# Four whole-array matmuls that nothing reads, at each level of the first ten triangular inverses

## The chip, the cores and the metric

The kernel runs on one NeuronCore of a Trainium2 chip. Its engines are TensorE (PE in the rows, with PEld for its weight loads), VectorE (DVE), ScalarE (ACT), GpSimd (POOL) and SyncE (SP), which issues the DMAs. The metric is the device time of one execution in microseconds. The kernel before takes 2458.19 us, the median of three runs that lie between 2457.12 and 2461.14 us.

## The reference

The reference is a two-layer backbone over 1024 latent and 256 context tokens of width 1024, in float32. Each layer normalizes and modulates its tokens, multiplies them by one input matrix, sends half of the columns through a retention group and half through an RWKV-7 group, gates both, multiplies by an output matrix and adds the result to the residual. What matters here is the recurrence of the RWKV group, which runs in both directions over 8 heads of 64 channels:

```python
def step(s, inp):
    r_t, w_t, k_t, v_t, kap_t, a_t = inp
    s_kap = jnp.einsum('bhvk,bhk->bhv', s, kap_t)
    s = (s * w_t[:, :, None, :]
         - s_kap[..., None] * (kap_t * a_t)[:, :, None, :]
         + v_t[..., None] * k_t[:, :, None, :])
    return s, jnp.einsum('bhvk,bhk->bhv', s, r_t)
```

The kernel computes it in chunks of 64 tokens. Within a chunk the recurrence is a triangular system, so each chunk needs the inverse of a 64x64 unit triangular matrix for every head and direction. That inverse depends on the inputs alone and not on the running state, so it can be made ahead of the scan.

## The kernel before

A layer has 4 pairs of heads (NP) and 10 steps (NT) for each pair. One step g covers 128 tokens, that is two chunks of 64 (index i) in two directions (index d) for two heads (index h), and the text below calls it a chunk, as the short description of the change does. So there are 40 chunks in a layer and 80 in the program. A chunk passes three functions:

- `prep` loads its features and makes the decayed vectors `own` and `bk`, mostly on DVE, ACT and POOL.
- `prep2` multiplies them (L962, tile `pm`), masks the products, and inverts the triangular part in six levels, n = 0 to 5, and three correction sums. The inverse lives in one bank of PSUM, the tile `pinv` of 512 columns (`pc` in the code). Its first half `q` takes the first products of a level (L1001: weights `hi`, moving operand `tz`, four matmuls with 64 columns each). DVE multiplies `q` by a mask into `xx` (L1015). The second half `tp` takes the second products (L1017: weights `ttb`, moving operand `xx`). ACT copies `tp` into the next `tz` (L1018), DVE turns it (L1021), ACT and POOL copy the result into `ttb` (L986), and the next level begins. After level 5 the sums of L990 and L993 follow. Two banks (LANES) let two chunks be inverted at a time.
- `seq` runs the recurrence itself over the chunk (L1053 and L1061, tile `pseq`).

Beside this scan a layer has a large amount of other PE work, which the text calls the fill: the input projections (L493 to L495), small products for the decay (L725), the retention group, and the output projection (L821 to L823). A generator hands out the fill in pieces. `ahead(g)` issues `prep` of chunk g and `prep2` of chunk g-1. At the start of a layer, `ahead` runs for g = 0 to LOOK (3), with 5 us of fill (RAMP) after each. From then on each step issues `seq`, `ahead(g + LOOK + 1)` and a share of the fill. All this fixes the order in which instructions are written down. A scheduler that simulates the engines then sets the order on each engine; `seq` and `prep2` stand under `tc.high_priority(offset=1000)`, so that it takes them before the fill where both are ready. On the chip each engine works through its list in that order.

Of the kernel before, what the change touches and what calls it, by code (L numbers as in the profile page):

```python
# [42 lines left out]
LOOK = 3  # L43
# [15 lines left out]
XB = 4  # L59
DENSE = ((447.0, 113.0), (403.0, 88.0))  # L60
DUE = (30, 37)


def shape_constants():
# [61 lines left out]
def hybrid_kernel(ctx: ExitStack, tc: tile.TileContext, a: dict, out: bass.AP, dbg: dict | None = None):  # L126
    nc = tc.nc
# [11 lines left out]
    def bank(tag, name):  # L139
        return ps.tile([128, 512], F32, tag=tag, name=name, bufs=BANKS[tag])  # L140
# [6 lines left out]
    def behind(ins, first):  # L147
        tc.add_manual_dep(ins.ins, first.ins.name, mybir.DependencyInfo(mybir.DependencyClass.NoSync, mybir.DependencyReason.DATA),
                          reason="the first product of a bank clears its written bits")
# [15 lines left out]
    def x_tile(tb):  # L165
        t = ln_pool.tile([128, D], F32, tag="xt", name="xt", bufs=XTB)
        load(t, a["ctx"][0, 128 * tb:128 * tb + 128, :] if tb < 2 else a["x"][0, 128 * (tb - 2):128 * (tb - 2) + 128, :])
        return t
# [20 lines left out]
    one16 = const.tile([128, 128], F16, name="one16")  # L189
# [37 lines left out]
    def turn(key):  # L227
        at[key] += 1
        return ring[key][(at[key] - 1) % len(ring[key])]
# [144 lines left out]
    for l in range(DEPTH):  # L374
# [55 lines left out]
        if l == 0:  # L430
            lp = ln_pool
            stage = [lp.tile([128, 8, 128 * len(tiles)], F32, name=f"xs{ci}") for ci, tiles in enumerate(LN_TILES)]
            for ci, tiles in enumerate(LN_TILES):
# [5 lines left out]
                for i, tb in enumerate(tiles):  # L439
                    t = x_tiles[tb] if tb < XTB else x_tile(tb)  # L440
# [7 lines left out]
                for k in range(8):  # L448
                    p = bank(("inv", "m")[k % 2], "pxt")
# [497 lines left out]
                nc.gpsimd.tensor_tensor(own[:, :, :, 64:128], rx, dt(exc(ep)), ALU.mult)  # L947
            return dict(s=s, uv=uv, f=f, own=own, bk=bk, skip_y=skip_y)

        def prep2(sp, c):  # L950
            own, bk, skip_y = c["own"], c["bk"], c["skip_y"]

            q1 = 64 if skip_y else 128
            gq = sp.tile([128, 2, 2, 2, 128], F32, tag="gq", name="gq", bufs=LIVE)
            bt = sp.tile([128, 2, 2, 128], F32, tag="bt", name="bt", bufs=LIVE)
            quad = lambda t: t.rearrange("p (i d t) -> p i d t", i=2, d=2)
            pm = {}
            for h in range(2):
                pm[h] = quad(bank("m", f"pm{h}"))
                for i in range(2):  # L960
                    for d in range(2):
                        nc.tensor.matmul(pm[h][:, i, d, 0:q1], bk[HR[h], i, d, :], own[HR[h], i, d, 0:q1],  # L962
                                         start=True, stop=True)
                for i in range(2):
                    nc.vector.tensor_tensor(gq[:, h, i, :, 0:q1], pm[h][:, i, :, 0:q1], m1mask[:, :, 0:q1], ALU.mult)  # L965
            pt = quad(bank("m", "pbt"))
            for i in range(2):
                for d in range(2):
                    nc.tensor.transpose(pt[:, i, d, :], bk[:, i, d, :], ident)
            nc.scalar.activation(bt, pt, AF.Copy, scale=rowf)  # L970

            hi, lo = turn("hi"), turn("lo")
            idb = ident[0:64, 0:64].unsqueeze(1).unsqueeze(1).to_broadcast([64, 2, 2, 64])
            il = sp.tile([128, 2, 2, 64], F32, tag="il", name="il", bufs=1)
            for h in range(2):
                nc.gpsimd.tensor_tensor(il[HR[h]], gq[0:64, h, :, :, 0:64], idb, ALU.add)  # L976
                nc.scalar.copy(hi[HR[h], :, :, 64 * h:64 * h + 64], il[HR[h]])  # L977
            lane = at["lane"] = (at["lane"] + 1) % LANES
            pc = bank("inv", "pinv")
            q, tp = [pc[:, 256 * k:256 * k + 256].rearrange("p (i d t) -> p i d t", i=2, d=2) for k in range(2)]  # L980
            ID = [(i, d) for i in range(2) for d in range(2)]
            idr = lambda t: t.rearrange("p i d t -> p (i d) t")

            def spread(dst, src):
                for h, eng in enumerate((nc.scalar.copy, nc.gpsimd.tensor_copy)):
                    eng(idr(dst[HR[h], :, :, 64 * h:64 * h + 64]), idr(src[HR[h]]))  # L986

            def one_sum(lhs, rhs, parts):

                one = nc.tensor.matmul(pc[:, 0:256], lhs, rhs, start=True, stop=False, skip_group_check=True)  # L990
                for n, (w, x) in enumerate(parts):
                    for i, d in ID:
                        behind(nc.tensor.matmul(q[:, i, d, :], w[:, i, d, :], x[:, i, d, :], start=False,  # L993
                                                stop=n == len(parts) - 1, skip_group_check=True), one)


            tz = ttb = tt = None
            for n in range(6):
                tzn = sp.tile([128, 2, 2, 64], F16, tag=f"tz{lane}", name="tz", bufs=2)
                for i, d in ID:  # L1000
                    nc.tensor.matmul(q[:, i, d, :], hi[:, i, d, :], id16 if n == 0 else tz[:, i, d, :], start=True, stop=True)  # L1001
                mk = lvm[:, :, n, :].unsqueeze(1).to_broadcast([128, 2, 2, 64])
                if n == 0:
                    nc.vector.tensor_tensor(tzn, q, mk, ALU.mult)
                    ttn = turn(f"ttb{lane}")
                    for d in range(2):
                        mt = lvm[:, 1 - d, 0, :].unsqueeze(1).unsqueeze(1).to_broadcast([128, 2, 2, 64])
                        nc.gpsimd.tensor_tensor(ttn[:, :, d, :].rearrange("p i (h t) -> p i h t", h=2),  # L1008
                                                hi[:, :, d, :].rearrange("p i (h t) -> p i h t", h=2), mt, ALU.mult)
                    for h in range(2):  # L1010
                        cols = slice(64 * h, 64 * h + 64)
                        nc.gpsimd.tensor_tensor(lo[HR[h], :, :, cols], il[HR[h]], hi[HR[h], :, :, cols], ALU.subtract)  # L1012
                else:
                    xx = sp.tile([128, 2, 2, 64], F16, tag=f"xx{lane}", name="xx", bufs=1)
                    nc.vector.tensor_tensor(xx, q, mk, ALU.mult)  # L1015
                    for i, d in ID:
                        nc.tensor.matmul(tp[:, i, d, :], ttb[:, i, d, :], xx[:, i, d, :], start=True, stop=True)  # L1017
                    nc.scalar.copy(tzn, tp)  # L1018
                    if n < 5:
                        tt = sp.tile([128, 2, 2, 64], F16, tag=f"tt{lane}", name="tt", bufs=1)  # L1020
                        nc.vector.transpose(idr(tt), idr(tzn))  # L1021
                        ttn = turn(f"ttb{lane}")
                        spread(ttn, tt)
                    else:
                        for d in range(2):
                            for h in range(2):
                                dn, up = [slice(64 * h + 32 * k, 64 * h + 32 * k + 32) for k in (1 - d, d)]
                                nc.vector.transpose(tt[up, :, d, 32 * (1 - d):32 * (1 - d) + 32], tzn[dn, :, d, 32 * d:32 * d + 32])
                tz, ttb = tzn, ttn
            one_sum(neg16, id16.unsqueeze(1).to_broadcast([128, 4, 64]), [(hi, tz), (lo, tz)])  # L1030
            e = turn("eb")
            for h in range(2):
                nc.scalar.activation(idr(e[HR[h], :, :, 64 * h:64 * h + 64]), idr(q[HR[h]]), AF.Copy, scale=-1.0)
            flat = lambda t: t.rearrange("p i d t -> p (i d t)")
            one_sum(one16, flat(tt), [(e, tt)])
            z1 = sp.tile([128, 2, 2, 64], F16, tag="z1", name="z1", bufs=1)
            nc.scalar.copy(z1, q)
            one_sum(one16, flat(tt), [(e, z1)])
            z2 = sp.tile([128, 2, 2, 64], F32, tag="z2", name="z2", bufs=ZB)
            nc.scalar.copy(z2, q)  # L1040
            c.update(gq=gq, bt=bt, z2=z2)
# [179 lines left out]
        def pump(w):  # L1221

            while w > 0 and fills:
                w -= take()

        def deal(g):

            n = len(fills)
            if n == 2 or (n == 1 and g >= DUE[0]):
                pump(left[-n] / max(DUE[-n] - g, 1))  # L1230

        def need(p, done):
            while p not in done:
                take()

        sp = open_pool("scan", other)
# [5 lines left out]
        stages, late = {}, {}  # L1242

        def ahead(g):
            p, s = divmod(g, NT)
            if p < NP:
                need(p, ready)
                stages[g] = prep(sp, p, s)
            if 0 <= g - 1 < NP * NT:
                with tc.high_priority(offset=1000):  # L1250
                    prep2(sp, stages[g - 1])

        for g in range(LOOK + 1):
            ahead(g)
# [2 lines left out]
        for p in range(NP):  # L1257
            st, ys = None, {}
            for s in range(NT):
                g = p * NT + s  # L1260
# [55 lines left out]
```

## Time and profile before

| | |
|---|---|
| time, median of 3 runs | 2458.19 us |
| the profiled execution, its own time | 2462.74 us |
| its span, first to last instruction | 2460.7 us |
| mean granted TensorE clock over the span | 0.964 of full speed |
| busy share of PE, DVE, ACT, POOL | 93%, 71%, 57%, 54% |
| DMA, mean over the span | 123 GB/s |

Line numbers are those of the kernel before. The busy time of PE counts a matmul from its start to its modelled end, so matmuls that follow one another closely overlap in it, and a stretch in which PE is shown as busy throughout can still run at either clock. A granted clock of 1.00 is 2.4 GHz and one of 0.50 is 1.2 GHz; a mean between the two is a stretch with some of both. A bracket at the end of a timeline row gives the idle time of the engine before that row and what ended it.

### The profile page before, as it was taken

Reading aid. Unit: us, or ns where it says so; the run is one execution under the profiler, and the core shown is the slowest. Engines: PE = TensorE matmul, PEld = TensorE weight load, DVE = VectorE, ACT = ScalarE, POOL = GpSimd, SP = SyncE. Lnnn points to the kernel's source line nnn. Section 1 sums busy time; section 2 is a strip of 40 time slices with the busy share of each in tenths; the row PEclk is TensorE's granted clock in tenths of the full one; section 3 lists DMA queues with packets and bytes.
Section 4 is the critical chain, followed back from the end, with each engine's and each line's share of the span. In section 5 each row is a group of like instructions: output and inputs, shape, how many; then the busy total and the mean of one; then the engine's idle time right before and its main releaser. Section 6 shows DMA issues by size and latency. Waiting matters only on the chain.

```text
span 2460.7 us, 69593 instructions
## 1 busy us (share of the span) xinstructions
PE 2299.2 (93%) x25463; PEld 1739.9 (71%) x25463; DVE 1735.6 (71%) x4784; ACT 1414.8 (57%) x4261; POOL 1319.7 (54%) x2032
## 2 busy tenths in 40 slices
PE   5779999999999999999997899999999999998997
PEld 2357776877788777778655687778768877776855
DVE  2646686787678867777648677767867886669756
ACT  3455664565566655456546666646655665456663
POOL 1455564465556654456536556545654665456662
PEclk7888999999999999999998899999999999999998
DMA  8754443334334423335533543434433443334544
GB/s 313 270 187 110 117 118 87 113 108 124 78 89 139 126 70 92 75 100 154 176 108 123 152 130 112 108 94 119 128 87 100 124 124 80 79 88 120 143 130 128
DMA packets 539606, 302.77 MB, mean 123 GB/s; under 512 B 238995, under 2 KB 526465, under 8 KB 537217
## 3 DMA queue, kind: packets, MB, share of 16 engines
q1 hardware_dynamic: 539264, 298.33, 42.1%
q8 instruction: 201, 3.29, 0.6%
q14 instruction: 141, 1.15, 0.2%
HBM read 212.21 MB, written 85.98 MB: 121 GB/s over the span
## 4 chain that ended last, share of the span: by engine, by line
PE 58%; DVE 13%; DMA 6%; ACT 4%; issue 3%; POOL 2%; SPq 2%; DVEq 0%; POOLq 0%; ACTq 0%
PE pproj L493 8%; PE pproj L495 8%; PE pproj L494 8%; PE pseq L1061 8%; PE pm L962 5%; DMA ft<-feat 2%; PE pseq L1053 2%; PE pinv L1001 2%; PE pinv L1017 2%; PE pout L821 1%; PE pout L823 1%; PE pss L638 1%; PE pout L822 1%; PE pss L648 1%; PE pyt L1127 1%
## 5 line engine op out<-in xcount | busy, mean ns | idle before, releaser
L493 PE MATMUL pproj<-h_hi,whi 128*128 128x256 f16 (+2 forms) x2128 | 631.3, 298 | 9.1 <-ACT craw L505 5.1
L494 PE MATMUL pproj<-h_lo,whi 128*128 128x256 f16 (+2 forms) x2128 | 629.1, 297 | 7.6 <-DVE h_lo L365 7.1
L495 PE MATMUL pproj<-h_hi,wlo 128*128 128x256 f16 (+2 forms) x2128 | 627.2, 297 | 0.7 <-POOL wlo L320 0.7
L320 POOL TENSOR_TENSOR wlo<-wraw,whi 128x256 f16<-128x256 f32 x360 | 250.5, 707 | 208.7 <-ACT wraw L319 181.0
L495 PEld LDWEIGHTS <-wlo 128*128 128x128 f16 x2128 | 213.5, 100 | 76.5 <-issue 12.1
L494 PEld LDWEIGHTS <-whi 128*128 128x128 f16 x2128 | 212.6, 100 | 77.6 <-issue 18.6
L493 PEld LDWEIGHTS <-whi 128*128 128x128 f16 x2128 | 213.1, 100 | 75.3 <-issue 10.4
L986 POOL COPY ttb<-tt 64x256 f16<-64x256 f16 x320 | 139.1, 436 | 205.2 <-DVE tt L1021 160.5
L1015 DVE TENSOR_TENSOR xx<-pinv,lvm 128x256 f16<-128x256 f32 x400 | 164.3, 416 | 90.6 <-PE pinv L1001 87.4
L318 ACT ACTIVATE whi<-wraw 128x256 f16<-128x256 f32 x360 | 139.2, 412 | 132.9 <-PE pproj L494 61.1
L1018 ACT CAST tz<-pinv 128x256 f16<-128x256 f32 x400 | 146.1, 370 | 119.9 <-PE pinv L1017 107.7
L962 PE MATMUL pm<-own,bk 64*128 64x128 f32 (+1 forms) x1280 | 201.6, 294 | 8.3 <-DVE bk L942 4.0
L1021 DVE STREAM_TRANSPOSE tt<-tz 128x256 f16<-128x256 f16 x320 | 139.4, 437 | 97.0 <-ACT tz L1018 94.3
L976 POOL TENSOR_TENSOR il<-gq,c_id 64x256 f32<-64x256 f32 x160 | 120.1, 751 | 133.1 <-DVE gq L965 119.3
L986 ACT COPY ttb<-tt 64x256 f16<-64x256 f16 x320 | 128.6, 402 | 106.5 <-DVE tt L1021 102.1
L962 PEld LDWEIGHTS pm<-own,bk 64*128 64x128 f32 x1280 | 163.2, 193 | 33.1 <-issue 8.6
L965 DVE TENSOR_TENSOR gq<-pm,c_m 128x256 f32<-128x256 f32 (+1 forms) x320 | 115.7, 402 | 50.6 <-PE pm L962 49.8
L1061 PE MATMUL pseq<-st,own 64*64 64x64 f32 x2432 | 149.4, 228 | 0.0
L319 ACT ACTIVATE wraw<-wraw 128x256 f32<-128x256 f32 x376 | 146.3, 410 | 3.9
L1001 PEld LDWEIGHTS <-hi 128*128 128x128 f16 x1920 | 104.6, 99 | 41.6 <-issue 9.7
L1012 POOL TENSOR_TENSOR lo<-il,hi 64x256 f16<-64x256 f32 x160 | 113.5, 710 | 36.8 <-ACT hi L977 28.0
L1008 POOL TENSOR_TENSOR ttb<-hi,lvm 128x256 f16<-128x256 f16 x160 | 113.6, 729 | 19.0 <-ACT hi L977 18.2
(255 smaller groups left out, 5906.7 us busy)
## 6 DMA issues: line engine op xcount, KB each, us to landing
ft<-feat SPq DMA_DIRECT2D x320, 160.0 KB
wraw<-in_w_in_dram SPq DMA_DIRECT2D x264, 128.0 KB
feat<-zth SPq DMA_DIRECT2D x80, 256.0 KB
wm<-in_w_mod_dram SPq DMA_DIRECT2D x16, 1024.0 KB
wraw<-in_w_out_dram SPq DMA_DIRECT2D x112, 128.0 KB
lap<-la SPq DMA_DIRECT2D x40, 256.0 KB
uv<-vt SPq DMA_DIRECT2D x320, 32.0 KB
wm<-in_w_mod_dram SPq DMA_DIRECT2D x16, 512.0 KB
```

What stands on the lines that cost most here:

```text
L319: nc.scalar.activation(raw, raw, AF.Copy, scale=WS)
L320: nc.gpsimd.tensor_tensor(lo, raw, hi, ALU.subtract)
L493: nc.tensor.matmul(p[:, 0:n], hi[:, k, :], h_hi[:, kk, m0:m1], start=first, stop=False)
L494: nc.tensor.matmul(p[:, 0:n], hi[:, k, :], h_lo[:, kk, m0:m1], start=False, stop=False)
L495: nc.tensor.matmul(p[:, 0:n], lo[:, k, :], h_hi[:, kk, m0:m1], start=False, stop=stop)
L962: nc.tensor.matmul(pm[h][:, i, d, 0:q1], bk[HR[h], i, d, :], own[HR[h], i, d, 0:q1], start=True, stop=True)
L986: eng(idr(dst[HR[h], :, :, 64 * h:64 * h + 64]), idr(src[HR[h]]))
L1001: nc.tensor.matmul(q[:, i, d, :], hi[:, i, d, :], id16 if n == 0 else tz[:, i, d, :], start=True, stop=True)
L1015: nc.vector.tensor_tensor(xx, q, mk, ALU.mult)
L1018: nc.scalar.copy(tzn, tp)
L1021: nc.vector.transpose(idr(tt), idr(tzn))
L1061: rm = nc.tensor.matmul(pq[HR[h], k, d, :], lhs, rhs, start=False, stop=stop, skip_group_check=True)
```

## The change

`prep2` gets a flag, and with it each of the levels 1 to 5 has four more matmuls behind its first products. Their weights are `one16`, a 128x128 identity in float16, and their moving operand is the whole of `tz`, 128x256 in float16. They write the second half of the bank, columns 256 to 511, which the second products of the same level overwrite later. Nothing reads what they write. The flag is set for g up to LOOK + 2 = 5, that is for the chunks 0 to 4 of each layer.

```diff
+KEEP = 4
...
-        def prep2(sp, c):
+        def prep2(sp, c, keep_clock=False):
...
                 for i, d in ID:
                     nc.tensor.matmul(q[:, i, d, :], hi[:, i, d, :], id16 if n == 0 else tz[:, i, d, :], start=True, stop=True)
+                if keep_clock and n:
+
+                    for _ in range(KEEP):
+                        nc.tensor.matmul(pc[:, 256:512], one16, tz.rearrange("p i d t -> p (i d t)"), start=True, stop=True)
                 mk = lvm[:, :, n, :].unsqueeze(1).to_broadcast([128, 2, 2, 64])
...
-                    prep2(sp, stages[g - 1])
+                    prep2(sp, stages[g - 1], g <= LOOK + 2)
```

On PE the built program has 200 matmuls and 200 weight loads more, and no other instruction is added or taken away on any engine. Behind the first of them the scheduler orders the rest of the program anew on all engines: on DVE the two lists differ from their 183rd instruction of 4722 on.

The first place is on PE, at level 1 of the first chunk of layer 0: `hi` and `ttb` are weights of the inverse, `one` those of the new matmuls, and the rows with `wz` belong to the fill. Before:

```order
L1001 LDWEIGHTS hi_1772
L1001 MATMUL pinv<-tz,hi_1772 128x64
L1017 LDWEIGHTS ttb_1786
L1017 MATMUL pinv<-xx,ttb_1786 128x64
L725 LDWEIGHTS wz
L725 MATMUL pz<-lh,wz 128x256
```

and after, with line numbers that are 1 higher up to L1002 and 5 higher from there on:

```order
L1002 LDWEIGHTS hi_1772
L1002 MATMUL pinv<-tz,hi_1772 128x64
L1006 LDWEIGHTS one_97
L1006 MATMUL pinv<-tz,one_97 128x256
L1006 LDWEIGHTS one_97
L1006 MATMUL pinv<-tz,one_97 128x256
L1006 LDWEIGHTS one_97
L1006 MATMUL pinv<-tz,one_97 128x256
L1006 LDWEIGHTS one_97
L1006 MATMUL pinv<-tz,one_97 128x256
L726 LDWEIGHTS wz
L726 MATMUL pz<-lh,wz 128x256
```

The four stand directly behind the first products, ahead of the fill. In the built program the mask multiplication `xx` of such a level waits for the semaphore value that the fourth of them sets; before, it waits for the value that the last first product sets.

The second place is on PE near the end of layer 1, in the inverse of the last chunk, between its second and its third correction sum. Before, output projections (`pout`) stand between the sums:

```order
L1053 MATMUL pseq<-uv,gq 64x64 x4
L1061 MATMUL pseq<-st,own 64x64 x4
L821 LDWEIGHTS wlh
L821 MATMUL pout<-mh,wlh 128x512
L822 LDWEIGHTS wlh
L822 MATMUL pout<-ml,wlh 128x512
L823 LDWEIGHTS wll
L823 MATMUL pout<-mh,wll 128x512
```

and after, the third sum follows with no fill ahead of it:

```order
L1132 MATMUL pyt<-c_id,yc 64x64 x8
L1058 MATMUL pseq<-uv,gq 64x64 x4
L1066 MATMUL pseq<-st,own 64x64 x3
L991 LDWEIGHTS one_97
L991 MATMUL pinv<-tt,one_97 128x256
```

From level 4 of that inverse to its third sum, about 14 us of output projections stood on PE before (by their columns, 256 of them in the time that the rows below show); now there are none, and they have moved ahead of it. Behind the third sum, 18 us of them are left before and 15 us after.

## Rows read from the trace of the kernel before

**Rows 1.** The page: busy times, and the granted clock in 40 slices.
```profile
PE 2299.2 (93%) x25463; PEld 1739.9 (71%) x25463; DVE 1735.6 (71%) x4784; ACT 1414.8 (57%) x4261; POOL 1319.7 (54%) x2032
...
PEclk7888999999999999999998899999999999999998
```
**Rows 2.** Stages: length, busy PE, PEld, DVE, ACT, POOL, then clock, DMA share, GB/s.
```profile
182.00:300.00 118.00, 108.62 (x1287) 90.50 (x1287) 77.22 (x204) 70.25 (x207) 68.09 (x102) 0.94 0.41 116
300.00:1030.00 730.00, 718.80 (x8344) 555.67 (x8343) 546.18 (x1544) 427.32 (x1295) 403.48 (x623) 1.00 0.37 102
1387.00:1500.00 113.00, 105.47 (x1148) 87.09 (x1149) 82.99 (x203) 74.64 (x215) 70.19 (x107) 0.92 0.45 126
1500.00:2160.00 660.00, 644.02 (x7420) 492.07 (x7420) 489.88 (x1374) 391.32 (x1202) 369.83 (x569) 1.00 0.38 104
```
**Rows 3.** Line 1001, 175 to 300 us: durations in ns, first and last start.
```profile
L1001 PE MATMUL pinv<-tz,hi x100: 189/193/261, 183.9 to 298.8; 128*128 128x64 f16 x100
```
**Rows 4.** PE's timeline (start, us): matmuls with 256 columns, at either clock.
```profile
185.54 0.27 PE L493 MATMUL pproj<-h_hi,whi 128*128 128x256 f16 x1
...
186.96 0.27 PE L494 MATMUL pproj<-h_lo,whi 128*128 128x256 f16 x1
...
223.08 0.42 PE L494 MATMUL pproj<-h_lo,whi 128*128 128x256 f16 x1
...
226.06 0.42 PE L493 MATMUL pproj<-h_hi,whi 128*128 128x256 f16 x1
```
**Rows 5.** PE's timeline, level 1 of the first chunk.
```profile
183.86 0.28 PE L1001 MATMUL pinv<-tz,hi 128*128 128x64 f16 x4
184.66 0.19 PE L1017 MATMUL pinv<-xx,ttb 128*128 128x64 f16 x1 [0.52 <-DVE xx L1015]
```
**Rows 6.** DVE's timeline, the same level.
```profile
184.18 0.42 DVE L1015 TENSOR_TENSOR xx<-pinv,lvm 128x256 f16<-128x256 f32 x1 [0.37 <-PE pinv L1001]
```
**Rows 7.** Low-clock stretches in the two ramps; columns as in rows 2.
```profile
200.40:203.80 3.40, 3.40 (x18) 2.37 (x18) 3.40 (x7) 2.09 (x6) 3.34 (x5) 0.52 0.13 35
217.80:227.60 9.80, 8.26 (x49) 6.50 (x48) 5.26 (x11) 3.13 (x10) 6.03 (x9) 0.50 0.39 95
302.90:306.30 3.40, 2.90 (x21) 2.04 (x20) 3.30 (x11) 2.10 (x7) 2.99 (x5) 0.51 0.15 46
1384.90:1398.40 13.50, 10.73 (x62) 8.16 (x59) 12.48 (x25) 8.94 (x24) 10.61 (x14) 0.50 0.25 80
1405.60:1412.30 6.70, 5.97 (x37) 4.20 (x35) 3.19 (x8) 2.94 (x8) 2.92 (x4) 0.50 0.69 204
```
**Rows 8.** PE's timeline: idle times by those stretches, and first products within them.
```profile
217.64 0.66 PE L778 MATMUL pvt<-c_id,pvc 128*128 128x128 f32 x2 [2.13 <-DVE pvc L508]
...
227.37 0.42 PE L1001 MATMUL pinv<-tz,hi 128*128 128x64 f16 x4
...
1387.45 0.40 PE L1001 MATMUL pinv<-id,hi 128*128 128x64 f16 x4 [1.90 <-ACT hi L977]
...
1390.60 0.40 PE L1001 MATMUL pinv<-tz,hi 128*128 128x64 f16 x4
...
1407.12 0.42 PE L1001 MATMUL pinv<-tz,hi 128*128 128x64 f16 x4
```
**Rows 9.** PE's timeline: an inverse with little fill beside it.
```profile
1400.66 0.28 PE L1001 MATMUL pinv<-tz,hi 128*128 128x64 f16 x4
...
1401.45 0.28 PE L1017 MATMUL pinv<-xx,ttb 128*128 128x64 f16 x4
1402.38 0.28 PE L1001 MATMUL pinv<-tz,hi 128*128 128x64 f16 x4 [0.66 <-ACT tz L1018]
1403.39 0.28 PE L1001 MATMUL pinv<-tz,hi 128*128 128x64 f16 x4 [0.72 <-ACT tz L1018]
```
**Rows 10.** PE's timeline: the last chunk's inverse, level 4 and third sum.
```profile
2390.17 0.28 PE L1001 MATMUL pinv<-tz,hi 128*128 128x64 f16 x4
...
2411.57 0.28 PE L993 MATMUL pinv<-z,eb 128*128 128x64 f16 x4
```

## The prediction

> **What bounds the kernel now.** I read the page first, then busy times by stage, then PE's timeline at the start and the end of the scan. On the page PE is busy for 93% of the span and the next engine, DVE, for 71%; PE's granted clock is below its full value mainly in the first slices and around the 22nd, where each layer's scan starts [rows 1]. By stage the kernel is plain: from 300 to 1030 us PE is idle for 11.2 of 730 us, from 1500 to 2160 us for 16.0 of 660 us, both at the full clock [rows 2]. There the kernel goes as fast as PE works through its list. In the two ramps, where the first chunks of a layer are inverted, PE is idle for 9.4 of 118 us and 7.5 of 113 us, and the mean clock is 0.94 and 0.92 [rows 2]. So these stages too are mostly PE's, with some idle time and some time at 1.2 GHz.
>
> The new matmuls stand in these ramps. In layer 0 the first products of the five chunks at the levels 1 to 5 are the 100 instructions that start between 183.9 and 298.8 us, four to a level, so 25 levels [rows 3]; layer 1 has as many, from 1390.6 us on [rows 8].
>
> **What is added on PE.** 2 layers x 5 chunks x 5 levels x 4 is 200 matmuls with 256 columns. The trace has many of that shape with the same kind of weights. From 185.54 to 186.96 us are 13 steps, so 0.109 us each at full clock; from 223.08 to 226.06 us are 14 steps, so 0.213 us at half [rows 4]. Their weight loads run beside the matmul ahead of them, as in those rows. A group of four is 0.44 us, the sum 21.8 us. Three of the 50 places lie in stretches at the low clock, at 227.37, 1390.60 and 1407.12 us [rows 8], where a group takes 0.85 us: 1.2 us more.
>
> **What the wait adds.** The built program lets the mask multiplication `xx` wait for the fourth new matmul and no longer for the last first product. At level 1 of the first chunk, `xx` starts 0.32 us after the first products and the second products follow 0.80 us after them [rows 5, 6]. The four end 0.44 us later than the first products, so `xx` moves by that, and with it the second products. This is why PE's idle time does not hide the four: the 0.52 us of idle ahead of the second products [rows 5] is a wait for `xx`, and it moves along. A group costs 0.44 us on PE where PE is full, and 0.44 us on the chain of levels where the chain is what PE waits for. Behind `xx` on DVE's queue stands `ll`, for which the fill's small products wait, and then the features of later chunks. DVE is idle for 40.8 of the 118 us [rows 2], and 25 x 0.44 us is 10.9 us, so I cost that delay at nothing; without the cover it would be those 10.9 us for each layer, but then in place of the time on PE and not on top.
>
> The Trainium skill says why this wait is there: by its page PSUM — Partial Sum Buffer, section "PSUM bank collisions raise a hardware error", two engines are to be kept apart by bank and quadrant, not by address, and the second half lies in the bank that DVE reads. By that rule a group in a chain-bound stretch costs its 0.44 us; if halves could be used at once it would be free there. No row of before shows the two together.
>
> What is hidden is bounded by nothing and by the ramps' idle time, 9.4 + 7.5 = 16.9 us. I take 2 us, near the lower end, for idle time that neither list nor chain sets (such as 2.13 us for a convolution of the fill [rows 8]).
>
> **What the clock can give back.** In the ramps PE is at 1.2 GHz in five stretches: 3.4, 9.8, 3.4, 13.5 and 6.7 us [rows 7]. The fourth begins at 1384.9 us, ahead of the first new matmul, which can come at 1390.6 us at the earliest [rows 8], so 7.8 us of it are in reach. That is 31.1 us in all; at the full clock a PE that never waits would need half, so 15.6 us is the most that there is to gain. The other end is a loss: one more stretch like that of 9.8 us would cost 4.9 us. The stretches come with idle time. Ahead of the second, PE waits 2.13 us for `pvc`; ahead of the fourth, just after the clock has fallen, 1.90 us for `hi`, before there is a level 1 at all [rows 8]. No first products of a level from 1 on stand in those two waits, so the new matmuls don't fill them. Ahead of the fifth it is another matter: first products at 1402.38 and 1403.39 us stand between waits of 0.66 and 0.72 us [rows 9], and two groups bring 0.87 us of whole-array work there. I take half of that stretch, 3.4 us, and a little more elsewhere: 4 us gained.
>
> The Trainium skill would have it go further: by TensorE: Matmul & The Clock Gate, section "HAM oscillation — how this bites in real kernels", idle gaps throttle PE again and the next burst begins cold, so filling gaps keeps the clock. The rows agree that idle time stands by each fall; if the rule worked at all five places, the gain would be those 15.6 us.
>
> **What the new order does.** The list is changed behind the first new matmul on all engines. Most of it I cannot price. One place stands out: near the end, the last chunk's inverse loses the 14 us of output projections beside it. Before, level 4 to the third sum takes 21.4 us [rows 10]. Alone, a level takes 0.79 + 0.93 = 1.7 us [rows 9]; two levels and three sums of a half level's length (0.9 us) are 6.1 us, and some products of the scan stand between. So I estimate 7 to 10 us for the inverse alone, and with the 14 us ahead of it 21 to 24 us against 21.4 us: 0 to 3 us lost. With 3 us less fill behind it, and a like stretch in layer 0, the term lies between -3 and +8 us; I take +3.
>
> **The sum.** 21.8 + 1.2 - 2 - 4 + 3 = 20 us. The profiled execution took 2462.74 us, 2.0 us of it outside its span of 2460.7 us, so it would become 2482.7 us. It stands 4.5 us above the median of the runs, 2458.19 us; the forecast for the median is 2478 us, 0.8% slower. Nothing later gives the time back in this forecast: in the dense stages PE works through a fixed list.
>
> **Rivals.**
> A, faster: the clock holds at every place in reach and the four fill idle time besides. The gain of 15.6 us and half of the idle time, 8.5 us, against 21.8 us is -2 us; with all 16.9 us it is -11 us. Taken at -7 us, this gives 2451 us. It decides from the point where clock and idle time together pass 21.8 us. For it speaks that each fall follows a gap [rows 7, 8]; against it that the two longest of those gaps hold no level from 1 on, and that `xx` moves with the four.
> B, taken up later: PE's idle time in the dense stages, 11.2 + 16.0 = 27.2 us [rows 2], is waits for other engines, and if PE comes later they have finished. Then most of the 20 us goes there, and the time is 2460 us. Against it: DVE and ACT wait for PE's products in turn and are late as well.
> C, much slower: the new order leaves the scan's ends uncovered in both layers. Two tails at 8 us each instead of 3 us together, no gain of clock and nothing hidden give 21.8 + 1.2 + 16 = 39 us, so 2497 us. For it speaks the second place in the order; against it that PE's total does not change.
>
> **How the numbers follow.** The forecast has a chance of 0.61, with a range of its own from 2466 to 2490 us; A has 0.13, B 0.12 and C 0.14. What a measurement of this kernel can tell from no change is about 0.2%, 4.9 us. So faster has 0.13 (A), within 0.2% has 0.11 (nearly all of B), and slower 0.76 (the forecast, C and the rest of B). The range of 2454 to 2497 us leaves out most of A and half of C.
>
> **What would show it.** In the changed kernel's trace, 200 matmuls at the new line with steps of 0.109 us, `xx` starting some 0.75 us after the first products of its level and waiting for that line, and PE's busy time in the ramps up by about 10 us each. The low stretches near 200 and 218 us, and the one from 1385 us, should still be there in some form, the one near 1406 us shorter or gone. Above 300 us the dense stages should be as long as before. I am wrong if the ramps end as early as before, if the mean clock of both ramps rises to 0.98 or more, or if a dense stage has become shorter or longer by over 8 us, since then the order decides and not the matmuls.

## The result, and the profile after

The changed kernel takes 2489.53 us (median of 4 runs, 2482.28 to 2498.66) against 2459.66 us for the kernel before in the same session (4 runs, 2457.12 to 2464.59): a ratio of 1.0113, 95% interval 1.0082 to 1.0145, so about 28 us slower by the ratio (the two medians lie 30 us apart; ratios and intervals here and below are those on record). 2478 us was forecast. Sign and range held, but the experiments show that two terms of the sum were wrong in opposite directions: the products cost far less than forecast, and the new order of the program far more.

Lines have moved: by one up to the first products (output projection 821 to 822, first products 1001 to 1002) and by five behind the new line 1006 (`xx` 1015 to 1020, second products 1017 to 1022). The profiled execution of the changed kernel took 2482.28 us, its span 2480.5 us. It was the quickest of its four, and that of the kernel before, 2462.74 us, lies 3 us above the median. So the two traces lie 20 us apart and can show only that much of the 28. First the page, for [rows 1]:

```profile
PE 2325.0 (94%) x25663; PEld 1752.6 (71%) x25663; DVE 1703.1 (69%) x4784; ACT 1416.3 (57%) x4261; POOL 1324.3 (53%) x2032
...
PEclk7889999999999999999998899999999999999997
```

PE has 200 instructions more and is busy for 25.8 us more. Now the stages of [rows 2], at the same times (length, busy PE, PEld, DVE, ACT, POOL, clock, DMA share, GB/s):

```profile
182.00:300.00 118.00, 110.76 (x1336) 92.30 (x1335) 77.56 (x200) 72.29 (x210) 66.11 (x102) 1.00 0.38 105
300.00:1030.00 730.00, 720.65 (x8320) 554.38 (x8320) 531.57 (x1534) 421.18 (x1287) 401.39 (x616) 1.00 0.38 103
1387.00:1500.00 113.00, 103.99 (x1072) 85.15 (x1070) 77.41 (x191) 69.00 (x192) 66.72 (x99) 0.91 0.47 127
1500.00:2160.00 660.00, 649.83 (x7525) 498.70 (x7525) 481.35 (x1378) 398.99 (x1220) 377.95 (x576) 0.99 0.39 107
```

In layer 0's first chunks PE did the 100 products and got through almost the old work besides, because the clock was 1.00 and no longer 0.94, and PE idle for 7.2 us in place of 9.4. Layer 1's first chunks are at 0.91, no better than before.

One level of the first chunk, on PE and then on DVE, answers to [rows 5, 6] (start, length, line, operation; in brackets the idle time before and its releaser):

```profile
186.34 0.28 PE L1002 MATMUL pinv<-tz,hi 128*128 128x64 f16 x4
186.45 0.60 PE L1006 MATMUL pinv<-tz,one 128*128 128x256 f16 x4
186.89 0.27 PE L726 MATMUL pz<-lh,wz 128*128 128x256 f16 x1
187.57 0.28 PE L1022 MATMUL pinv<-xx,ttb 128*128 128x64 f16 x4 [0.41 <-DVE xx L1020]
```

```profile
187.09 0.42 DVE L1020 TENSOR_TENSOR xx<-pinv,lvm 128x256 f16<-128x256 f32 x1 [0.81 <-PE pinv L1006]
```

The four take 186.89 - 186.45 = 0.44 us, and `xx` starts 0.75 us after the first products: the price and the wait are those of the forecast.

What was not forecast stands at the ends of the layers. I added up the columns that PE has streamed (float32 counted four times, the added products left out) and read from the records when each kernel had got through the same sum. By that count the profiled execution was 1.8 us behind at 366.5 us, 5.6 us behind at 1283.6 us, and 17.0 us behind at 1423.7 us: 11 us went between the last scan steps of layer 0 and the first of layer 1. It was 12.3 us behind at 2408.3 us, and the last 60 us lost 8 more. In the first of these stretches PE waits in another place than before. Before:

```profile
PE prsb L345 <- POOL rs L250: 5.7, 1, 5.7
PE pxo L890 <- ACT osq L892: 3.5, 2, 3.3
PE pproj L493 <- ACT craw L505: 3.1, 3, 1.7
PE pout L821 <- DVE x L824: 2.6, 5, 1.2
```

and after (engine, line, waited for: us in total, times, longest):

```profile
PE pout L822 <- DVE x L825: 7.9, 6, 2.3
PE pout L822 <- ACT mh L812: 5.7, 1, 5.7
PE pinv L1002 <- ACT tz L1023: 2.3, 1, 2.3
```

The output projection of the layer's last tiles now runs into the wait for the mix that comes back from memory (`mh`) and for the sum `x`. The longest wait stands where the loss is largest. The same work took 12.0 us before and takes 17.7 us after (columns as in [rows 2]):

```profile
1278.00:1290.00 12.00, 11.46 (x85) 6.42 (x83) 6.11 (x16) 6.99 (x21) 4.16 (x6) 1.00 0.73 224
```

```profile
1283.60:1301.30 17.70, 10.10 (x110) 5.50 (x107) 9.79 (x29) 7.07 (x22) 6.00 (x8) 0.74 0.74 222
```

PE is idle for 7.6 us there in place of 0.5, 5.7 of it in the one wait for `mh`, and the clock falls in that wait. Over the whole stretch, 128.7 us before and 140.1 after, idle time is 33.0 us in place of 27.5 and time at the low clock 43 us in place of 28.5. Half of those 14 us is 7 us, an estimate of what the clock costs, so the 11 us are lost to the waits and to the clock in about equal parts.

In the last 70 us the matmuls of the output projection (`pout`) alone are these, in the kernel before (length, busy PE, busy DVE, then clock, DMA share and GB/s of the whole stretch):

```profile
2390.70:2460.70 70.00, 35.03 (x183) 16.27 (x28) 0.90 0.41 126
```

and after:

```profile
2410.50:2480.50 70.00, 23.64 (x130) 13.91 (x25) 0.78 0.36 112
```

53 of the 183 matmuls, 11 us of cover for the last scan steps, had been done earlier, and the clock is 0.78 in place of 0.90. Level 4 and the third sum of the last chunk's inverse, for [rows 10]:

```profile
2413.26 0.29 PE L1002 MATMUL pinv<-tz,hi 128*128 128x64 f16 x4
...
2424.12 0.42 PE L994 MATMUL pinv<-z,eb 128*128 128x64 f16 x4
```

From the one to the other take 10.9 us in place of 21.4 us, with the output projection gone from between them. The third sum is 12.6 us later than before, as late as the kernel was already; from it to the end of the span are 56.4 us in place of 49.1 us. The 7 us are lost behind the inverse. These are the two ends, before and after (columns as in [rows 2]):

```profile
2411.57:2460.70 49.13, 34.75 (x339) 24.85 (x336) 33.93 (x93) 15.01 (x45) 7.61 (x12) 0.86 0.43 134
```

```profile
2424.12:2480.50 56.38, 39.31 (x343) 26.92 (x341) 34.85 (x94) 16.23 (x47) 6.87 (x11) 0.77 0.26 92
```

PE's idle time is 17.1 us in place of 14.4 there, and its time at the low clock 25.7 us in place of 14.2. Half of those 11.5 us is some 6 us, so the clock is the larger part of the loss: it fell at 2418.4 us, inside the bare inverse, and rose again at 2435.5 us. Less fill behind the third sum is not the cause. By the traces 117 matmuls of the output projection stand there before and 120 after, 15.0 and 15.7 us by their columns, and not 18 and 15 us as the section on the change has it.

### The profile page after: what moved, and what is told of

Its sections match the earlier page's. It is cut to its first block, busy times and chain, and to the rows that moved or that the text cites. A ratio compares the mean times of both kernels' runs of the same rounds, so it can differ in the third digit from the quotient of the medians.

```text
span 2480.5 us, 69894 instructions
## 1 busy us (share of the span) xinstructions
PE 2325.0 (94%) x25663; PEld 1752.6 (71%) x25663; DVE 1703.1 (69%) x4784; ACT 1416.3 (57%) x4261; POOL 1324.3 (53%) x2032
## 4 chain that ended last, share of the span: by engine, by line
PE 70%; DVE 9%; DMA 5%; issue 3%; ACT 3%; POOL 2%; SPq 2%; DVEq 0%; POOLq 0%; ACTq 0%
PE pproj L494 9%; PE pproj L496 9%; PE pproj L495 9%; PE pseq L1066 9%; PE pm L963 6%; PE pseq L1058 2%; PE pinv L1002 2%; PE pinv L1022 2%; PE pout L822 2%; PE pout L824 2%; PE pout L823 2%; PE pss L639 2%; DMA mraw<-mix 1%; DMA ft<-feat 1%; PE pss L642 1%
## 5 line engine op out<-in xcount | busy, mean ns | idle before, releaser
L1002 PEld LDWEIGHTS <-hi 128*128 128x128 f16 x1920 | 102.5, 99 | 38.0 <-issue 8.0
```

## The experiments

Two causes had to be told apart, the products and the new order. The program was therefore edited behind the scheduler, instruction by instruction: all engines' queues and all waits stay as they are, and only the products (a weight load and a matmul each) are put in or taken out, with the semaphore count of the last of a group moved to the instruction that is then the last. The cuts below show the edits in short, with comments for what is left out. That gives the two missing corners of old or new order, with or without products. "Old order" is that of the kernel before.

**The new order without the products.**

```diff
     with _tile.TileContext(nc, schedule_with_timeline_sim=True) as tc:
         hybrid_kernel(tc, args, outs[0])
+    # the 200 products of line 1006 and their weight loads go, their counts to the last first product
+    blk.instructions = [swap.get(k, i) for k, i in enumerate(L) if k not in gone]
```

> Leaves out the 200 added products (and their weight loads) from the changed program and keeps everything else of it, every engine's order and every wait. Theory P (the products themselves take the time: 200 x 0.109 us on TensorE, less what idle time and the clock give back): back to before, 2456 to 2464 us, ratio to before 0.998 to 1.002. Theory O (the products nearly pay for themselves, as the lag of the changed kernel at equal TensorE work says: 0 at the end of layer 0's first chunks and only 3 us more over layer 1's; the new order costs the rest): 2474 to 2486 us, ratio 1.006 to 1.011, and the low clock of before near 200 and 218 us is back. Both in halves: about 2470.

Measured: 2478.16 us (6 runs) against 2463.70 us, ratio 1.0077 (1.0051 to 1.0104): 19 us, between 13 and 26 (the medians lie 14.5 us apart). The order alone costs about two thirds of the change, or half by the medians. Its end looks like that of the changed kernel; `pout` in the last 70 us:

```profile
2402.90:2472.90 70.00, 23.29 (x128) 13.90 (x25) 0.76 0.36 112
```

One part of the expectation failed: the low clock of layer 0 did not come back in full (3.4 us of it between 180 and 310 us, 17.1 us in the kernel before).

**The old order with the products.**

```diff
+    # behind the last first product of levels 1 to 5, chunks 0 to 4 of each layer
+    out.append(swap.get(k, i))      # this product, without its semaphore count
+    out += after.get(k, [])         # 4 x (load one16, multiply tz), the last with that count
```

> The kernel before with every engine's order and waits as they were, and the four products put into TensorE's row behind the last first product of levels 1 to 5 of chunks 0 to 4 of both layers; the mask multiply waits for the fourth of them. Theory P: 2474 to 2484 us, ratio 1.006 to 1.010. Theory O: 2456 to 2466 us, ratio 0.998 to 1.003, with no low clock between 190 and 300 us. If the two add up, this difference and that of the bare new order together make the change's own 1.13%.

Measured: 2469.49 us (12 runs), ratio 1.0024 (1.0005 to 1.0043): 6 us, between 1 and 11, of the 21.8 us that PE spends. With the bare order's 0.77% this makes 1.01%, inside the interval of the whole change. The expectation of no low clock between 190 and 300 us failed: 6.8 us of it are left. The tail is the old one, `pout` in the last 70 us:

```profile
2396.70:2466.70 70.00, 34.78 (x183) 15.94 (x28) 0.90 0.41 127
```

and both ramps have a higher clock than before, 0.97 and 0.94 in place of 0.94 and 0.92 [rows 2]:

```profile
182.00:300.00 118.00, 109.79 (x1286) 91.18 (x1285) 75.96 (x195) 69.80 (x203) 65.00 (x99) 0.97 0.38 104
...
1387.00:1500.00 113.00, 104.97 (x1123) 87.08 (x1122) 80.14 (x195) 71.64 (x203) 66.31 (x99) 0.94 0.44 122
```

**One layer at a time**, both in the old order:

```diff
-    4 if n and g % 40 < 5 else 0
+    4 if n and g < 5 else 0          # layer 0 alone
+    4 if n and 40 <= g < 45 else 0   # layer 1 alone
```

> The old order, with the products in layer 0 alone (100). Theory P: half of the change, 2466 to 2472 us, ratio 1.003 to 1.005. Theory O: the clock that layer 0 keeps (17 us at half speed, 8.5 us) pays for the 10.9 us of products: 2456 to 2463 us, ratio 0.9985 to 1.0015.

> The old order, with the products in layer 1 alone (100). Theory P: 2466 to 2472 us, ratio 1.003 to 1.005. Theory O: no clock is kept there (20.5 us of low clock in both kernels near 1385 to 1420 us), so 10.9 us less what idle time hides: +3 to +8, 2462 to 2468 us, ratio 1.001 to 1.003.

Measured: layer 0 alone 2462.78 us (12 runs), ratio 0.9993 (0.9974 to 1.0013); layer 1 alone 2466.17 us (12 runs), ratio 1.0026 (1.0009 to 1.0043). A hundred products, 10.9 us, cost nothing that can be measured in layer 0 and about 6 us (2 to 11) in layer 1.

**Eight in place of four**, in the old order at all 50 levels:

```diff
-    4 if n and g % 40 < 5 else 0
+    8 if n and g % 40 < 5 else 0
```

> The old order and waits with eight products in place of four at the same 50 levels (400 in all). Theory linear: each further product costs what the first four did in the old order (+0.24% for 200), plus what idle time no longer hides, so +0.5% to +1.0%: 2476 to 2488 us. Theory clock: eight products fill the wait on the mask multiply, layer 1's first chunks keep the clock as well (20 us of low clock there before), and the second four cost nothing: +0.1% to +0.35%.

Measured: 2495.58 us (5 runs), ratio 1.0132 (1.0099 to 1.0166). Neither theory: the second four cost 27 us, with an uncertainty of some 10 us, where the first four cost 6 us; they take 21.8 us on PE. At equal work its trace falls behind by 10 us in layer 0's first chunks, by 18 us from 1288 to 1564 us, and by some 10 us more from 2260 to 2433 us. So what pays for most of the first four pays for little or nothing of the second.

**Other orders, without products.** The same source with one, two or eight products a level, or with four in one layer alone, was given to the scheduler, and all products were then taken out again. Only the order differs from the kernel before.

```diff
-KEEP = 4
+KEEP = 1                             # also 2, 8
-                    prep2(sp, stages[g - 1], g <= LOOK + 2)
+                    prep2(sp, stages[g - 1], last and g <= LOOK + 2)       # layer 1 alone
+                    prep2(sp, stages[g - 1], not last and g <= LOOK + 2)   # layer 0 alone
+    # then every product out, as above
```

> The order that the scheduler makes when it is given one product at each of the 50 levels, with all products left out again. Theory tied (the order is bad because the scheduler makes room for products): a quarter of the bare order of four's +0.77%, so +0.0% to +0.25%. Theory draw (any edit gives another order, and the old one is a good one among them): not tied to the number, +0.3% to +1.2%, with the loss again at the ends of the layers.

> The order that the scheduler makes for eight products a level, all left out again. Theory tied: about twice the bare order of four, +1.2% to +1.8%. Theory draw: anywhere from 0 to +1.2%, no larger than that of four by rule.

> The order that the scheduler makes when it is given four products a level in layer 1 alone, all left out again: as before up to the first chunks of layer 1, other behind them. Theory ends (the new order of four loses 8 to 9 us between the end of layer 0's chunks and layer 1's and as much in the last 60 us, which the traces show beside equal work): the first loss is gone, so half of it, +0.3% to +0.5%, if its tail is as bad, and 0 if it is not. Against it: +0.7% or more, which would put the cost into layer 1's dense stages.

> The order that the scheduler makes for two products a level at the 50 levels, all left out. Bare orders of 1, 4 and 8 stand at +0.35%, +0.77% and +1.35%. Theory tied: between 1 and 4, +0.45% to +0.6%. Theory draw: the number decides nothing, and any value from 0 to +1.4% can come, with most of it at the end of layer 0 (gap between its last and layer 1's first scan step: 140 us in the old order, 149 to 152 in those of 1 and 4) and in the last 70 us (183 to 191 out-projection products there in the quick tails, 121 to 128 in the slow ones).

> The order that the scheduler makes when it is given four products a level in layer 0 alone, all left out again. The bare order of layer 1 alone stood at +0.75%, as much as that of both layers. Theory tied: the two layers' parts add up to both layers' +0.77%, so about 0 here. Theory draw: another order with ends of its own, +0.3% to +1.0%, and the sum of the two need not be that of both; its loss can be read from the gap at the end of layer 0 and from the count of out-projection products in the last 70 us.

Two of these orders are only in part new. Matmul by matmul, that of layer 1 alone is the order of the kernel before up to 1394 us, and that of layer 0 alone is the order of four up to 1398 us.

Measured, with the length of two stretches of equal work (in the kernel before 1278.0 to 1406.7 us and 2396.0 to 2453.7 us) and the `pout` matmuls in the last 70 us, from the profiled executions. "Low" is an estimate of the time at the lower clock, 2 x (1 - mean clock) x span, as a mean over all runs on record, beside that of the kernel before in the same session; its standard error is 3 to 7 us. Each ratio is against the kernel before in its own session:

| order made for | median us (runs) | ratio (95%) | end of layer 0 | last scan steps | `pout` | low, us (before) |
|---|---|---|---|---|---|---|
| none (before) | 2463.70 | 1 | 128.7 | 57.7 | 183 | 183 |
| none, with 4 products | 2469.49 (12) | 1.0024 (1.0005 to 1.0043) | 129.9 | 57.3 | 183 | 169 (183) |
| 1 a level | 2469.39 (11) | 1.0035 (1.0014 to 1.0055) | 136.8 | 56.4 | 185 | 185 (181) |
| 2 a level | 2489.75 (5) | 1.0120 (1.0091 to 1.0150) | 129.3 | 66.1 | 141 | 210 (179) |
| 4 a level | 2478.16 (6) | 1.0077 (1.0051 to 1.0104) | 137.9 | 65.9 | 128 | 201 (183) |
| 8 a level | 2495.23 (5) | 1.0135 (1.0100 to 1.0170) | 129.5 | 67.5 | 130 | 230 (181) |
| 4, layer 0 alone | 2473.84 (11) | 1.0063 (1.0043 to 1.0084) | 139.1 | 67.8 | 127 | 187 (179) |
| 4, layer 1 alone | 2482.62 (10) | 1.0075 (1.0051 to 1.0099) | 131.8 | 68.2 | 123 | 222 (181) |

The theory that the cost grows with the number of products has against it two a level, which came out above four (their intervals overlap a little), and the two layers alone, which do not add up; eight a level lay where it had them (1.2% to 1.8%) and above the other theory's 1.2%. That of layer 1 alone was put at 0.3% to 0.5% if the ends were all, and cost 0.75%. The orders fall into two kinds at each end: 129 to 132 us or 137 to 139 us at the end of layer 0, and 56 to 58 us or 66 to 68 us in the last scan steps, where the long kind always has fewer `pout` matmuls left. The order of four has drawn the long kind at both ends, 8 to 9 us each, which is nearly all of its 19 us; that of layer 0 alone, whose profiled execution was the slowest of its eleven (2491.49 us), has both too, the first because it is the same order there. Those of two, of eight and of layer 1 alone (which is the old order there) are as quick as before at the end of layer 0, and lose 10 to 16 us in the work that the kernel before does between 1536 and 2396 us as well. In the profiled executions that loss is mostly the clock's: their time at the low level in this work is 41, 72 and 68 us, against 24 us in the kernel before. The last column says the same of all runs: the order of layer 1 alone has 41 us more at the low level, which at half is all of the 19 us that it costs, and that of four 17 us more, about half of its 19 us. `pout` in the last 70 us of the order for layer 1 alone:

```profile
2415.20:2485.20 70.00, 21.70 (x123) 14.12 (x25) 0.77 0.33 106
```

**A thrifty version**, the old order with two products in the first two chunks of layer 0, where the clock was low before:

```diff
-    4 if n and g % 40 < 5 else 0
+    2 if n and g < 2 else 0
```

> The old order with two products at levels 1 to 5 of chunks 0 and 1 of layer 0 (20 in all, 2.2 us), where before had its low clock near 200 and 218 us. If these few keep the clock as the hundred in layer 0 did (10 us less low clock up to 365 us), 3 us quicker than before, -0.1%; if they don't, +0.05%. Both are close to what five rounds can tell from nothing.

Measured: 2461.90 us (12 runs), ratio 1.0002 (0.9979 to 1.0025), against 2457.56 us in that session. Low clock between 180 and 310 us was 3.4 us, but the time cannot be told from no change: 7 us less at the low level in the stretch near 218 us is worth 3.5 us at most, and the products take 2.2 us. No version beat the kernel before.

## Why the prediction came out as it did

**What is added on PE, and the wait: right.** 0.44 us a group, `xx` 0.75 us after the first products and waiting for the new line, as forecast. In the changed kernel that wait is what ends DVE's idle time 18 times, 11.3 us in all:

```profile
DVE xx L1020 <- PE pinv L1006: 11.3, 18, 1.5
```

The rule of the Trainium skill (PSUM — Partial Sum Buffer, "PSUM bank collisions raise a hardware error") that two engines be kept apart by bank agrees with that wait, 0.75 us in place of 0.32 us; a version in which `xx` does not wait was not tried.

**"I take 2 us" hidden and "4 us gained" by the clock: both too small.** The forecast for the products was 21.8 + 1.2 - 2 - 4 = 17 us; in the old order they cost 6 us (1 to 11). The clock explains a good part. In the old order, low clock between 180 and 310 us was 17.1, 12.7 and 19.9 us in three profiled executions without products there (the third is the order for layer 1 alone), 9.0, 8.8 and 6.8 us with four or eight a level, and 3.4 us in the thrifty version; between 1375 and 1440 us it was 20.5, 23.9 and 20.5 us without and 13.7, 17.1 and 13.7 us with. That is some 8 us less in layer 0 and 7 us in layer 1, worth half of it, together 7 to 8 us. All runs bear out the sum, 169 us at the low level in place of 183, a difference of 14 with an uncertainty of 11. In layer 1 it came as forecast: with four products the stretch near 1406 us is gone, and that from 1385 us stays (1390.5 to 1404.2 us in the old order with products). In layer 0 it did not: the stretch that lasts from 217.6 to 227.9 us, 10.3 us in each of the three executions without products, is 3.4, 3.4, 6.8 and 3.4 us long in the four with them. So the step that failed is the argument that products which don't stand in the waits ahead of a fall can't change it, and the clock gave back 7 to 8 us in place of 4. The rest of what is hidden, 21.8 - 6 - 7 = 9 us with an uncertainty of some 7, in place of 2, I could not place. The Trainium skill's rule that filled gaps keep the clock (TensorE: Matmul & The Clock Gate, "HAM oscillation — how this bites in real kernels") agrees with the sign of this, not with its full reach: low clock became less, but 9.0 and 13.7 us of it are left in the two ramps.

The signs that the forecast gave failed in layer 0: the low stretches near 200 and 218 us are gone in the changed kernel. Layer 1's ramp kept its 20.5 us of low clock:

```profile
200.00:240.00 40.00, 35.73 (x410) 30.30 (x409) 28.95 (x69) 24.20 (x69) 21.13 (x34) 1.00 0.39 104
...
1400.00:1440.00 40.00, 33.93 (x295) 27.63 (x292) 26.46 (x63) 26.32 (x72) 21.31 (x30) 0.77 0.41 119
```

But the bare new order has 3.4 and 20.5 us in the same places, so in the changed kernel this is the order's doing as much as the products'.

**"What the new order does ... I take +3": the term that failed.** It measured 19 us (13 to 26), outside its bounds of -3 to +8. The place was named, the last chunk's end without output projections beside it, but I priced it by the inverse alone. That price was about right: 7 to 10 us were estimated for the inverse by itself, it took 10.9 us, and next to nothing was lost up to its third sum. The loss comes behind it: the clock falls in the bare inverse and stays low for 17.1 us, over the scan steps behind it, and the idle time of the last steps grows by 2.7 us. For that I had set only "3 us less fill behind it", and that reading was wrong, since as much fill stands there as before. The like stretch in layer 0, which I counted with the 3 us, cost 11 us by itself, about half of it in waits and half by the clock.

**Why the total still fell into the range.** 17 + 3 was forecast and 6 + 19 came; a sum of 20 against 25, and 28 (20 to 36) for the change itself. The forecast was right by errors that cancel, not by its reason. Rival C named the mechanism, two uncovered ends at 8 us each; its other half, no gain of clock and nothing hidden, did not come. The test that I set myself did fire: layer 0's ramp ended as early as before (366.5 against 364.7 us), "since then the order decides and not the matmuls". Rival A is out as a forecast of this change, but holds in layer 0 of the old order to the extent that a hundred products cost nothing there that can be measured. Rival B is not needed: the changed kernel regained 8 us between 1536 and 2396 us, but so did the bare order in part (4 us), and single executions of the kernel before differ by more than that.

What stays open is why the scheduler's other orders spend the output projection earlier, and whether moving those matmuls alone would mend the ends; at the end of layer 1 the traces show the two together in every order, and no run moved only them. Open is also why the orders of two, of eight and of layer 1 alone lose clock in layer 1's dense work.

## What to carry to other kernels

Where a scheduler places the instructions, an edit has two prices: the work, and another order for all that follows. Look in the new order for what covers the ends of the long dependent stages, and price all that has lost its cover, to the very end. One run with the new order and without the edit's work tells the two prices apart. A mean clock on record for every run shows, without a trace of each, how much of a price is clock.

## What the runs showed of the hardware that was not expected

In the tail of the changed kernel the clock fell to its lower level with no long idle time ahead of it. The last of the output projections there ended at about 2412.7 us. From 2412.6 us to the fall at 2418.4 us PE was busy for 3.73 of 5.8 us with 81 matmuls, nearly all of them small ones of the scan and the inverse, and the longest recorded wait is 1.2 us. At the low clock it was then busy for 13.68 of 17.1 us. The stretches before, at and behind the fall:

```profile
2412.60:2418.40 5.80, 3.73 (x81) 2.99 (x80) 4.48 (x16) 2.52 (x8) 2.08 (x4) 1.00 0.95 256
2418.40:2435.50 17.10, 13.68 (x132) 9.04 (x127) 8.69 (x32) 4.42 (x13) 2.81 (x4) 0.50 0.39 99
2435.50:2450.00 14.50, 14.25 (x163) 10.13 (x162) 12.27 (x35) 4.84 (x14) 0.72 (x2) 1.00 0.16 55
```

And the clock is not the same from one execution to the next: in the work that the kernel before does between 873.7 and 1112.1 us its profiled execution had 20.5 us of low clock, and three others of the old order (with products in both layers, with eight, and the thrifty version) had 20 to 24 us and took 238 to 240 us for it as well, while three more of the same order there (layer 0 alone, layer 1 alone, and the bare order for layer 1 alone) had none and took 230 us. So a difference of 8 to 10 us between two single profiled executions of this kernel can be chance, unless it repeats in others at the same place, as the losses at the layers' ends do.
